# Two-block transformer kernel on one core: low query parts on 128 rows, pools at multiples of 128 bytes, one table load placed later

## The chip, the cores and the metric

The kernel runs on one core of a Trainium2 chip. A core has five engines that run beside each other, each with its own queue: TensorE (PE in the profile, with its weight loads shown apart as PEld), VectorE (DVE), ScalarE (ACT), GpSimd (POOL) and SyncE (SP, which issues most DMAs). Operands lie in SBUF, a memory of 128 partitions; matmul results lie in PSUM. The metric is the device time of one execution in microseconds, as the median of several runs.

## The reference

Two transformer blocks run one after the other on 512 tokens (and 256 context tokens in the first). Everything is float32. The first block has a gated delta network, a SwiGLU feed-forward, a differential attention and a second feed-forward. The second block has a layer with sliding-window and stick-breaking attention and a layer with a chunked recurrence (HGRN2), each followed by cross attention to 256 memory tokens and a feed-forward with a short convolution. The part that the change edits most is the differential attention:

```python
# q, k: two halves of 64 for each of 8 heads; keys of 512 tokens and 256 of the context
s = einsum('cbhqd,cbhkd->cbhqk', q, k)          # c = 0, 1: the two halves
p = softmax(s, axis=-1)
a = p[0] - lam_val * p[1]
o = einsum('bhqk,bhkv->bhqv', a, v)
out = rms_norm(o, subln_g) * (1 - lambda_init)  # then  w_out
# recurrence (HGRN2): log_f = log(lb + (1 - lb) * sigmoid(f_logit)); k = (1 - lb) * sigmoid(-f_logit)
```

## The kernel before

**Rounded pairs.** Nearly all products are made from operands that are split into a rounded high part and a low part (type F32R, fp32r in the profile): `h*h + h*l + l*h`, three matmuls instead of one float32 matmul. `weights` (L200 to L204) loads a raw weight unit `wr` of 128x1024 by DMA from SP, ScalarE casts it to `wh` (L203), VectorE subtracts to get `wl` (L204). Activations are split in the same way into tiles such as `h2h`/`h2l`, `h3h`/`h3l`, `fh`/`fl`, `f1h`/`f1l`, `b1h`/`b1l`. Every matmul goes through `mm` (L163), every transposition through `tr` (L167, with the identity `ident`), so the tile names tell them apart. One matmul streams 512, 384 or 256 columns of the moving operand past 128x128 stationary values. In the profile the first tile name of a matmul is the moving one, the second the stationary one: in `f1h,wh` an activation of 512 tokens moves past a 128x128 block of weights, in `wh,fh` 512 columns of weights move past a 128x128 block of the activation.

**Differential attention** (`diff_attention`, tiles of pool `da`). `project(pr)` makes keys, queries and values of a pair of heads. `ev_k` applies the rotation (`rope`, L1113 to L1116, which uses a tile `rot`) into the buffer `kraw` and splits it: for each half `cc` the tile `kx` holds the high part on the own 64 rows and the low part on the other 64. `ev_q` makes the rotated queries in a tile `qraw` and fills `q` of three planes: planes 0 and 1 hold, for each half, the high part on the own 64 rows and a second copy of it on the other 64 (L1130, L1131); plane 2 holds the low parts of both halves (L1132). So a score tile is made of two matmuls for each of four (half, key range) combinations: one over 128 rows, high times (high and low), and one over 64 rows, low times high:

```python
self.mm(s[cc][:, f, 0:384], q[:, cc, t * P:(t + 1) * P], kx[:, cc, fs], stop=False)
self.mm(s[cc][:, f, 0:384], q[cp, 2, t * P:(t + 1) * P], kx[cp, cc, fs], start=False)
```

There are 8 heads of 4 token tiles with 8 such matmuls, 256 in all, half of them over 64 rows. `attend` then takes maxima (L1182), exponentials (L1185), mixes the two halves (L1192), transposes the result (`a<-ident,p`) and multiplies with `v` (`o<-v,aT`). `head_norm_out` (L1228 to L1236) normalises a head in the tile `ho`. While one pair of heads is attended, `take` fills in matmuls of the next pair's projections, and in the last pair matmuls of the output projection. On each engine the instructions run in one order, which the build's planner fixes beforehand from the program's priorities.

**Pools.** SBUF tiles come from pools that are stacked from the left and from the right end of each partition. Tiles lie one behind the other in their pool at their own size. In the program as built, the left side begins at byte 16,512 of a partition (129 times 128) with the pool `const` of 5,728 bytes (44 times 128 and 96), so what lies behind it starts 96 bytes past a multiple of 128. The right side ends at byte 229,344 (96 past a multiple of 128), and the pool `ada` of 928 bytes below it leaves the next pools 64 past a multiple. Small tiles of one or a few numbers lie between large ones in several pools. Two of the operand pairs below: `wh` and `wl` lie at 64 past a multiple of 128 and `fh` of the last feed-forward too, `f1h` at 96 past; `h3h` lies at 64, and the normalised memory and queries of the cross attention (`mh`, `q0h`) lie at 0.

**Recurrence** (`hgrn_mixer`). L1873 takes an exponential of a 128x16 tile, `exp_ln_tables` (L160) loads ScalarE's table for exponential and logarithm, L1882 takes a logarithm `lno` of 128x8, and then for each 128 channels `ev_f` (L1928 to L1942) takes an absolute value, an exponential and a logarithm of 128x512.

Of the kernel before, what the change touches and what calls it, by code (L numbers as in the profile page):

```python
# [12 lines left out]
F32 = mybir.dt.float32  # L13
# [8 lines left out]
P = 128  # L22
D = 1024
NK = D // P
SEQ = 512
CTX = 256
TOK = SEQ + CTX
NT = SEQ // P
# [12 lines left out]
class Kernel:  # L41
# [19 lines left out]
    def __init__(self, ctx, tc, ins, out):  # L61
        self.ctx, self.tc, self.nc, self.i, self.out = ctx, tc, tc.nc, ins, out
        self.n = 0
        self.staged = []
        self.turns, self.rest = {}, None
        self.ada_own = 0


    def pool(self, name, bufs=1, space=None, side=None):
# [5 lines left out]
        return self.tc.alloc_tile_pool(name=name, bufs=bufs, reuse_waits="tile", **kw)  # L75
# [31 lines left out]
    def setup(self):  # L107
        nc = self.nc
        self.c = self.pool("const", side="left")
# [280 lines left out]
    def deltanet(self, xp, xT, scratch, zs, gts, later):  # L390
# [43 lines left out]
        hp = self.pool("dn_heads", side="right")  # L434
# [46 lines left out]
        pp = self.pool("dn_proj", side="left")  # L481
# [602 lines left out]
    def diff_attention(self, hh, hl, yh, yl, sb, spare, later, after):  # L1084
# [26 lines left out]
        def rope(dst, ps):  # L1111
            rot = one([P, SEQ], "rot", 1)
# [5 lines left out]
        def project(pr, out):  # L1118
# [4 lines left out]
            def ev_q(j, ps):  # L1123

                raw = one([P, SEQ], "qraw")
                rope(raw, ps[0])
                q[j] = one([P, 3, SEQ], "q", 2, F32R)
                for cc in range(2):
# [3 lines left out]
                    nc.vector.tensor_tensor(out=q[j][own, 2, :], in0=raw[own], in1=q[j][own, cc, :].bitcast(F32), op=SUB)  # L1132
# [34 lines left out]
        def attend(h, q, kx, v, work, steps):  # L1167
            po = self.bank("o")
            r0 = one([P, NT], "r0", 2)
            for t in range(NT):  # L1170
                s = [self.bank2() for _ in range(2)]
                for cc in range(2):
                    cp = slice(64 * cc, 64 * cc + 64)
# [122 lines left out]
    def first_block(self):  # L1296
        nc, i = self.nc, self.i
        self.ap = self.pool("ada", side="right")
        self.aw = self.pool("adaw", side="right")
        xp = self.pool("dn_x", side="right")  # L1300
        self.stage = self.pool("stage", 2, side="right")
# [111 lines left out]
        sb = self.pool("da", side="left")  # L1413
# [22 lines left out]
        sb.release()  # L1436
# [14 lines left out]
        self.stage = self.pool("stage", 2, side="right")  # L1451
# [83 lines left out]
    def ab_mixer(self, hh, hl, yh, yl, sb, done_h, fill):  # L1535
# [7 lines left out]
        at = self.pool("swa", side="right")  # L1543
# [8 lines left out]
        prep = self.pool("prep", side="right")  # L1552
# [53 lines left out]
        swp = self.pool("swt", side="right")  # L1606
# [80 lines left out]
        at = self.pool("stick", side="right")  # L1687
# [174 lines left out]
    def hgrn_mixer(self, hh, hl, yh, yl, sb, done_h, fill):  # L1862
# [18 lines left out]
        self.exp_ln_tables()  # L1881
        nc.scalar.activation(lno, olb, AF.Ln)  # L1882
# [34 lines left out]
        def project(pr):  # L1917
# [6 lines left out]
            def ev_f(j, ps):  # L1924
# [3 lines left out]
                nc.scalar.activation(a, ps[0], AF.Abs)  # L1928
# [331 lines left out]
```

## Time and profile before

| | us |
|---|---|
| median of 3 runs (3797.12 to 3800.86) | 3800.17 |
| the profiled execution's own time | 3806.98 |
| its span, first to last instruction | 3805.3 |
| PE busy in the span | 3681.0 (97%) |
| DVE, ACT, POOL busy | 2338.4, 1540.7, 436.5 |

The profile gives each engine's busy time, lines of instructions grouped by their place in the code, the chain of work that ended last, and a timeline in which a row is a start, a duration, the engine, the line and the tiles. A matmul's duration runs from its start to its modelled end in PSUM, and successive matmuls overlap; what one costs in a dense stretch is the distance from its start to the next one's start, called its step below. `PEclk` is the clock that TensorE was granted, 1.00 being 2.4 GHz.

### The profile page before, as it was taken

To read this page: it belongs to the slowest core of one execution; us is meant where nothing else is said; L and a number is where in the kernel's file an instruction comes from. 1 tells how busy PE (TensorE), PEld (TensorE's weight loads), DVE (VectorE), ACT (ScalarE), POOL (GpSimd) and SP (SyncE) were. 2 spreads that over 40 slices of the span, in tenths; PEclk is the share of its full clock that TensorE was granted. 3 is DMA by queue.
4 is the path that set the end of the run, shared out by engine and by line. 5 is a ranking of instruction groups with operands and counts; after the bars stand their busy time and mean duration, and the time that the engine had idled before them with its cause. 6 is when DMAs were issued, how large, how long until landed. Compare 5 with 4: busy or idle time off the path is not lost.

```text
span 3805.3 us, 57443 instructions
## 1 busy us (share of the span) xinstructions
PE 3681.0 (97%) x23195; PEld 3032.8 (80%) x23195; DVE 2338.4 (61%) x3919; ACT 1540.7 (40%) x2834; POOL 436.5 (11%) x642
## 2 busy tenths in 40 slices
PE   8999998999999999999999999999999999999999
PEld 5776777888888787777888877888887878888887
DVE  4757765633444766677555656556666776556665
ACT  4445444321111344443222456543334555444332
POOL 3112220130000110003000202100001122100000
PEclk8999999999999999999999999999999999999999
DMA  4234334422222211113333213223232223212322
GB/s 168 89 98 143 116 120 145 136 67 61 67 62 61 74 45 40 45 40 108 95 94 100 78 53 98 63 66 100 89 100 78 78 68 102 93 61 89 95 94 83
DMA packets 246667, 329.44 MB, mean 87 GB/s; under 512 B 12103, under 2 KB 192683, under 8 KB 246400
## 3 DMA queue, kind: packets, MB, share of 16 engines
q1 hardware_dynamic: 245696, 325.39, 27.2%
q8 instruction: 182, 2.98, 0.3%
q14 instruction: 85, 0.70, 0.1%
q0 software_dynamic: 704, 0.37, 0.0%
HBM read 318.09 MB, written 7.63 MB: 86 GB/s over the span
## 4 chain that ended last, share of the span: by engine, by line
PE 82%; DVE 7%; ACT 4%; POOL 3%; DMA 2%; issue 2%; SPq 0%; ACTq 0%; POOLq 0%; DVEq 0%
PE g L163 41%; PE a L163 14%; PE o L163 13%; PE s L163 7%; PE i L163 2%; DMA araw<-in_ada_w_dram 1%; PE s L167 1%; PE a L167 1%; PE p L163 1%; DVE wl L204 1%; ACT wh L203 1%; ACT xr L1476 1%; ACT Wt L721 0%; DVE bst L964 0%; ACT xr L1473 0%
## 5 line engine op out<-in xcount | busy, mean ns | idle before, releaser
L204 DVE TENSOR_TENSOR wl<-wr,wh 128x1024 fp32r<-128x1024 f32 (+1 forms) x508 | 585.4, 1160 | 441.7 <-ACT wh L203 428.0
L203 ACT CAST wh<-wr 128x1024 fp32r<-128x1024 f32 (+1 forms) x508 | 493.4, 980 | 768.7 <-PE o L163 386.7
L163 PE MATMUL g<-wh,fh 128*128 128x512 f32 x396 | 156.4, 396 | 0.0
L163 PE MATMUL g<-wh,fl 128*128 128x512 f32 x396 | 156.0, 395 | 0.0
L163 PE MATMUL g<-wl,fh 128*128 128x512 f32 x396 | 155.1, 392 | 0.0
L163 PE MATMUL g<-h2l,wh 128*128 128x512 f32 x352 | 138.0, 392 | 2.5 <-DVE h2l L1010 2.5
L163 PE MATMUL g<-h2h,wh 128*128 128x512 f32 x352 | 137.5, 392 | 0.0
L163 PE MATMUL g<-h2h,wl 128*128 128x512 f32 x352 | 137.2, 390 | 0.0
L152 POOL TENSOR_SCALAR brs<-bmv 128x1 f32<-128x1 f32 x20 | 9.7, 484 | 937.1 <-DVE bmv L966 928.0
L163 PE MATMUL g<-hh,wh 128*128 128x512 f32 (+1 forms) x376 | 112.4, 358 | 3.4 <-ACT hh L417 1.6
L163 PE MATMUL g<-hl,wh 128*128 128x512 f32 (+1 forms) x376 | 111.0, 354 | 1.8 <-POOL hl L418 1.7
L163 PE MATMUL g<-hh,wl 128*128 128x512 f32 (+1 forms) x376 | 110.2, 354 | 1.7 <-DVE wl L204 1.7
L1045 DVE TENSOR_TENSOR x<-g,x 128x512 f32<-128x512 f32 x120 | 82.5, 688 | 31.0 <-PE g L163 30.8
L163 PE MATMUL s<-k,q 128*128 128x384 f32 (+1 forms) x256 | 98.7, 440 | 0.0
L1182 DVE TENSOR_REDUCE nm<-s 128x1 f32<-128x768 f32 x64 | 61.1, 955 | 52.4 <-PE s L163 52.3
L163 PEld LDWEIGHTS g<-wh,fh 128*128 128x128 f32 x396 | 74.4, 188 | 17.4 <-ACT fh L2092 0.6
L1287 ACT CAST fh<-sg 128x768 fp32r<-128x768 f32 (+1 forms) x44 | 32.0, 727 | 139.0 <-DVE sg L1286 139.0
L163 PEld LDWEIGHTS g<-wl,fh 128*128 128x128 f32 x396 | 74.4, 188 | 16.6
L163 PEld LDWEIGHTS g<-wh,fl 128*128 128x128 f32 x396 | 74.4, 188 | 16.4 <-DVE fl L2093 0.4
L1286 DVE TENSOR_TENSOR sg<-g,sg 128x512 f32<-128x512 f32 x33 | 22.8, 691 | 98.0 <-PE g L163 98.0
L163 PEld LDWEIGHTS g<-hh,wh 128*128 128x128 f32 x376 | 62.7, 193 | 24.7 <-issue 9.3
L163 PEld LDWEIGHTS g<-hh,wl 128*128 128x128 f32 x376 | 62.5, 192 | 23.7 <-issue 13.2
(992 smaller groups left out, 11541.2 us busy)
## 6 DMA issues: line engine op xcount, KB each, us to landing
wr<-in_ffn_w_up_dram SPq DMA_DIRECT2D x132, 512.0 KB, 3.6
araw<-in_ada_w_dram SPq DMA_DIRECT2D x48, 1024.0 KB, 5.2
wr<-in_ffn_w_down_dram SPq DMA_DIRECT2D x88, 512.0 KB, 3.7
wr<-in_ffn_w_gate_dram SPq DMA_DIRECT2D x44, 512.0 KB, 3.8
wr<-in_dn_w_in_dram SPq DMA_DIRECT2D x66, 256.0 KB, 4.4
wr<-in_xa_w_kv_dram SPq DMA_DIRECT2D x32, 512.0 KB, 3.5
wr<-in_hgrn_w_in_dram SPq DMA_DIRECT2D x32, 512.0 KB, 3.8
wr<-in_da_w_in_dram SPq DMA_DIRECT2D x24, 512.0 KB, 3.5
```

The costliest lines, as they stand in the source:

```text
L152: nc.gpsimd.tensor_scalar(out=out, in0=in_, scalar1=mul, scalar2=add, op0=MUL, op1=ADD)
L163: self.nc.tensor.matmul(out, lhsT=lhsT, rhs=rhs, start=start, stop=stop)
L167: self.nc.tensor.transpose(out, in_, self.ident[0:k, 0:k])
L203: nc.scalar.copy(hi, raw)
L204: nc.vector.tensor_tensor(out=lo, in0=raw, in1=hi.bitcast(F32), op=SUB)
L1045: nc.vector.tensor_tensor(out=a, in0=ps, in1=a, op=ADD)
L1182: nc.vector.tensor_reduce(out=nm, in_=s[cc][:, :, 0:384], axis=AX.XY, op=MAX, negate=True)
L1286: nc.vector.tensor_tensor(out=s, in0=p[:, 0:n], in1=s, op=MUL)
L1287: nc.scalar.copy(hi[j], sg[j])
L1476: nc.scalar.activation(y, x, AF.Copy, scale=rs)
```

## The change

It does three things, and some that these need.

1. In the differential attention, `q` gets four planes: the low part of each half has a plane of its own, with zeros (set by GpSimd) on the other 64 rows, and the low matmul runs over 128 rows. The tile `qraw` is gone, its work is done in `kraw`; the tile `rot` is gone, its work is done in a buffer of the tag `ho`.
2. Pools are brought to multiples of 128 bytes (32 numbers). `const` and `ada` get 32 and 64 bytes of padding. In pools that are not marked `packed`, each tile's size is rounded up to 128 bytes; in the pools `da`, `mix` and `xa`, tiles under 32 numbers go to a small pool beside.
3. In the recurrence, the table load and the logarithm `lno` come behind the first absolute value in `ev_f`.

```diff
+LINE = 32
     def t(self, pool, shape, tag, dt=F32, bufs=None):
+
         self.n += 1
-        return pool.tile(shape, dt, tag=tag, name=f"{tag}_{self.n}", bufs=bufs)
+        name = f"{tag}_{self.n}"
+        n = math.prod(shape[1:])
+        if n < LINE:
+            pool = self.small.get(id(pool), pool)
+        if id(pool) in self.packed or n % LINE == 0:
+            return pool.tile(shape, dt, tag=tag, name=name, bufs=bufs)
+        x = pool.tile([shape[0], -(-n // LINE) * LINE], dt, tag=tag, name=name, bufs=bufs)[:, 0:n]
...
+    def pool_pair(self, name, side):
+
+        pool = self.pool(name, side=side)
+        self.small[id(pool)] = self.pool(name + "s", side=side, packed=True)
+        return pool
...
+    def fill_lines(self, pool, n):
+
+        pad = self.t(pool, [P, n], "pad")
+        self.nc.gpsimd.memset(pad, 0.0)
...
-        self.c = self.pool("const", side="left")
+        self.c = self.pool("const", side="left", packed=True)
+        self.fill_lines(self.c, 8)
...
         def rope(dst, ps):
-            rot = one([P, SEQ], "rot", 1)
+            rot = one([P, NT, P], "ho", 1).rearrange("p t d -> p (t d)")
...
-                raw = one([P, SEQ], "qraw")
+
+                raw = kraw[:, 0:SEQ]
                 rope(raw, ps[0])
-                q[j] = one([P, 3, SEQ], "q", 2, F32R)
+                q[j] = one([P, 4, SEQ], "q", 2, F32R)
...
-                    nc.vector.tensor_tensor(out=q[j][own, 2, :], in0=raw[own], in1=q[j][own, cc, :].bitcast(F32), op=SUB)
+                    nc.gpsimd.memset(q[j][other, 2 + cc, :].bitcast(F32), 0.0)
+                    nc.vector.tensor_tensor(out=q[j][own, 2 + cc, :], in0=raw[own], in1=q[j][own, cc, :].bitcast(F32), op=SUB)
...
-                        self.mm(s[cc][:, f, 0:384], q[cp, 2, t * P:(t + 1) * P], kx[cp, cc, fs], start=False)
+                        self.mm(s[cc][:, f, 0:384], q[:, 2 + cc, t * P:(t + 1) * P], kx[:, cc, fs], start=False)
...
-        self.ap = self.pool("ada", side="right")
+        self.ap = self.pool("ada", side="right", packed=True)
+        self.fill_lines(self.ap, 16)
...
-        sb = self.pool("da", side="left")
+        sb = self.pool_pair("da", "left")
...
-        self.exp_ln_tables()
-        nc.scalar.activation(lno, olb, AF.Ln)
...
                 nc.scalar.activation(a, ps[0], AF.Abs)
+                if k == 0:
+                    self.exp_ln_tables()
+                    nc.scalar.activation(lno, olb, AF.Ln)
                 nc.scalar.activation(a, a, AF.Exp, scale=-1.0)
```

## Rows read from the trace of the kernel before

**Rows 1.** The page: span, busy time of each engine, chain that ended last.
```profile
span 3805.3 us, 57443 instructions
PE 3681.0 (97%) x23195; PEld 3032.8 (80%) x23195; DVE 2338.4 (61%) x3919; ACT 1540.7 (40%) x2834; POOL 436.5 (11%) x642
...
PE 82%; DVE 7%; ACT 4%; POOL 3%; DMA 2%; issue 2%; SPq 0%; ACTq 0%; POOLq 0%; DVEq 0%
```

**Rows 2.** Busy time by stretches: us, then each engine's busy, clock, DMA share, GB/s.
```profile
1357.00:1700.00 343.00, 336.20 (x1916) 267.39 (x1915) 224.85 (x419) 161.47 (x333) 17.61 (x24) 0.99 0.13 41
1640.00:1700.00 60.00, 56.76 (x276) 41.84 (x277) 39.47 (x79) 30.50 (x72) 3.96 (x6) 0.91 0.06 18
1760.00:2000.00 240.00, 240.00 (x1071) 197.46 (x1071) 133.03 (x153) 63.08 (x76) 6.40 (x7) 1.00 0.33 98
2700.00:2900.00 200.00, 200.00 (x865) 162.31 (x864) 135.57 (x180) 63.83 (x85) 0.00 (x0) 1.00 0.30 95
```

**Rows 3.** Score matmuls by form, 1357 to 1700: count, busy us, mean ns.
```profile
L163 PE MATMUL s<-k,q 64*128 64x384 f32 x128 | 57.3, 447 | 0.0
L163 PE MATMUL s<-k,q 128*128 128x384 f32 x128 | 55.4, 433 | 0.0
```

**Rows 4.** Weight loads in time, one half's scores: start, duration, idle before.
```profile
1401.22 0.19 PEld L163 LDWEIGHTS g<-wl,h3h 128*128 128x128 f32 x1
1401.35 0.46 PEld L167 LDWEIGHTS a<-ident,p 128*128 128x128 f32 x4
1401.78 0.19 PEld L163 LDWEIGHTS s<-k,q 128*128 128x128 f32 x1
1402.16 0.18 PEld L163 LDWEIGHTS s<-k,q 64*128 64x128 f32 x1 [0.18 <-issue]
1402.53 0.19 PEld L163 LDWEIGHTS s<-k,q 128*128 128x128 f32 x1 [0.19 <-issue]
1402.90 0.18 PEld L163 LDWEIGHTS s<-k,q 64*128 64x128 f32 x1 [0.19 <-issue]
1403.27 0.20 PEld L167 LDWEIGHTS a<-ident,p 128*128 128x128 f32 x2 [0.19 <-issue]
```

**Rows 5.** Timeline of PE in the last feed-forward, 512 columns.
```profile
3720.23 0.39 PE L163 MATMUL g<-wl,fh 128*128 128x512 f32 x1
...
3722.27 0.39 PE L163 MATMUL o<-wl,fh 128*128 128x512 f32 x1
3722.49 0.40 PE L163 MATMUL g<-f1h,wh 128*128 128x512 f32 x1
...
3726.00 0.40 PE L163 MATMUL g<-f1h,wh 128*128 128x512 f32 x1
```

**Rows 6.** Timeline of PE, 256 columns: values projection, then cross attention's queries.
```profile
1400.02 0.28 PE L163 MATMUL g<-wh,h3h 128*128 128x256 f32 x1
...
1401.34 0.28 PE L163 MATMUL g<-wl,h3h 128*128 128x256 f32 x1
...
2435.27 0.28 PE L163 MATMUL g<-wl,q0h 128*128 128x256 f32 x1
...
2449.40 0.28 PE L163 MATMUL o<-wl,q0h 128*128 128x256 f32 x1
```

**Rows 7.** Timeline of PE: the first and the last of the dense rounded matmuls.
```profile
37.99 0.51 PE L163 MATMUL g<-hh,wl 128*128 128x512 f32 x2
...
3799.93 0.39 PE L163 MATMUL o<-wh,fl 128*128 128x512 f32 x1
```

**Rows 8.** Timeline of PE: two plain float32 matmuls of 512 columns, operands at 0.
```profile
118.72 1.02 PE L163 MATMUL i<-gi,gt 128*128 128x512 f32 x2
```

**Rows 9.** The same form's durations, min/median/max in ns.
```profile
L163 PE MATMUL i<-gi,gt x32: 377/537/595, 118.7 to 513.0; 128*128 128x512 f32 x16, 128*128 128x256 f32 x16
```

**Rows 10.** Timeline of POOL and ACT in the recurrence: a 128x512 fill, the table loads.
```profile
2931.82 0.53 POOL L1885 MEMSET keep<- 128x512 f32 x1
...
2941.81 1.28 ACT L1873 ACT_TABLE_LOAD   x1
2943.11 0.21 ACT L1873 ACTIVATE lexp<-lexp 128x16 f32<-128x16 f32 x1
2943.34 1.28 ACT L160 ACT_TABLE_LOAD   x1
2944.63 0.21 ACT L1882 ACTIVATE lno<-olb 128x8 f32<-128x8 f32 x1
2944.83 0.60 ACT L1928 ACTIVATE fa<-g 128x512 f32<-128x512 f32 x1
```

**Rows 11.** The chain that ended last, around one head's normalisation.
```profile
1417.52 0.70 DVE ho L1228
...
1424.35 0.63 PE a L167 x4
```

More of the change, by code (lines that the diff above doesn't have):

```diff
@@ L64, in __init__, with pool @@
         self.staged = []
+        self.packed, self.small = {}, {}
         self.turns, self.rest = {}, None
         self.ada_own = 0
-    def pool(self, name, bufs=1, space=None, side=None):
+    def pool(self, name, bufs=1, space=None, side=None, packed=False):
         kw = {}
@@ L433, in deltanet @@
         self.ada_own = self.ada_bufs
-        hp = self.pool("dn_heads", side="right")
+        hp = self.pool("dn_heads", side="right", packed=True)
         one = lambda shape, tag, bufs=1, dt=F32: self.t(hp, shape, tag, dt, bufs)
@@ L480, in deltanet @@
         W2 = SEQ + 4 + CTX
-        pp = self.pool("dn_proj", side="left")
+        pp = self.pool("dn_proj", side="left", packed=True)
         onep = lambda shape, tag, bufs=1: self.t(pp, shape, tag, F32, bufs)
@@ L1297, in first_block @@
         nc, i = self.nc, self.i
-        self.ap = self.pool("ada", side="right")
-        self.aw = self.pool("adaw", side="right")
-        xp = self.pool("dn_x", side="right")
-        self.stage = self.pool("stage", 2, side="right")
+        self.ap = self.pool("ada", side="right", packed=True)
+        self.fill_lines(self.ap, 16)
+        self.aw = self.pool("adaw", side="right", packed=True)
+        xp = self.pool("dn_x", side="right", packed=True)
+        self.stage = self.pool("stage", 2, side="right", packed=True)
         self.ada_setup()
@@ L1435, in first_block @@
         ln.release()
-        sb.release()
+        self.release_pair(sb)
         yTp.release()
@@ L1450, in first_block @@
         g, b = self.load_bc(ln, i["ln2_g"][1], "g"), self.load_bc(ln, i["ln2_b"][1], "b")
-        self.stage = self.pool("stage", 2, side="right")
+        self.stage = self.pool("stage", 2, side="right", packed=True)
         self.load_ffn_cols()
@@ L1542, in ab_mixer @@
         vb = one([P, NT, 512], "vb")
-        at = self.pool("swa", side="right")
+        at = self.pool("swa", side="right", packed=True)
         on = lambda shape, tag, bufs=1, dt=F32: self.t(at, shape, tag, dt, bufs)
@@ L1551, in ab_mixer @@
         va = on([P, NT, P], "va")
-        prep = self.pool("prep", side="right")
+        prep = self.pool("prep", side="right", packed=True)
         pr = lambda shape, tag, bufs=1, dt=F32: self.t(prep, shape, tag, dt, bufs)
@@ L1605, in ab_mixer @@
         self.exp_ln_tables()
-        swp = self.pool("swt", side="right")
+        swp = self.pool("swt", side="right", packed=True)
         on = lambda shape, tag, bufs=1, dt=F32: self.t(swp, shape, tag, dt, bufs)
@@ L1686, in ab_mixer @@
         at.release()
-        at = self.pool("stick", side="right")
+        at = self.pool("stick", side="right", packed=True)
         on = lambda shape, tag, bufs=1, dt=F32: self.t(at, shape, tag, dt, bufs)
@@ L2110, in second_block @@
             yTp, yh, yl = self.new_h(f"my{l}", SEQ, "right")
-            sb = self.pool("mix", side="right")
+            sb = self.pool_pair("mix", "right")
             kv = []
@@ L2122, in done_h @@
                 kvp = self.pool("kv", side="left")
-                mp = self.pool("memh", side="left")
+                mp = self.pool("memh", side="left", packed=True)
                 kT = self.t(kvp, [P, NK, 256], "mkT")
@@ L2152, in second_block @@
             yTp, yh, yl = self.new_h(f"cy{l}", SEQ, "right")
-            sb = self.pool("xa", side="right")
+            sb = self.pool_pair("xa", "right")
             w_o, part = i["xa_w_o_2"][l], self.xa_part
```

18 lines of the change are left out of this document (14 added, 4 removed).

## Prediction

> **What bounds the kernel now.** I read the page first. TensorE is busy for 3681.0 of 3805.3 us, no other engine for more than 61%, and the chain that ended last lies on PE for 82% [rows 1]. A busy PE need not be an efficient one, because matmuls overlap, so I then read stretches: in two feed-forwards PE has no idle time at all while DVE is busy for 133.03 of 240 us and 135.57 of 200 us, and in the differential attention PE is busy for 336.20 of 343 us with DVE at 224.85 [rows 2]. So what shortens the distance between matmul starts shortens the kernel, up to the point where VectorE or a chain through it comes last. The timeline of PE gives that distance, in two places where the change works.
>
> First, the scores. The table by form shows 128 matmuls over 64 rows and 128 over 128 rows, with 447 and 433 ns from start to modelled end [rows 3]. The weight loads show their steps: 1401.78, 1402.16, 1402.53, 1402.90, 1403.27, that is 372 ns from one to the next, and before each the weight loader is idle for 0.18 to 0.19 us with nothing that the profile can name [rows 4]. The loads before them, all over 128 rows, have no such gap. Here the forms alternate 128, 64, 128, 64. A change of rows thus seems to make the load wait for the matmul before it: 0.19 idle and 0.18 load is the whole step.
>
> Second, the dense rounded matmuls. With 512 columns, the nine steps from 3720.23 to 3722.27 take 226.7 ns each, and the 15 from 3722.49 to 3726.00 take 234.0 ns, on the same engine at the full clock, one after the other, with nothing waited for [rows 5]. In the first stretch both operands lie 64 bytes past a multiple of 128; in the second, the moving one lies 96 past. With 256 columns, 11 steps from 1400.02 to 1401.34 take 120.0 ns (both at 64), and 120 steps from 2435.27 to 2449.40 take 117.8 ns (moving at 64, stationary at 0) [rows 6]. One column per cycle at 2.4 GHz would be 213.3 and 106.7 ns. So 226.7 is 213.3 and 13.4, 120.0 is 106.7 and 13.3: the excess does not grow with the columns, and it is just 32 columns, or 128 bytes, of the moving operand. That is what reading one more piece of 128 bytes (17 for 16, 9 for 8) would cost. No rounded operand moves from a multiple of 128 anywhere in this kernel, so the trace has no row of the state after.
>
> **The sum, part by part.** All against the profiled execution (3806.98 us, span 3805.3 us).
>
> *Alignment.* I counted the steps between successive rounded matmuls over the whole timeline, from 37.99 to 3799.93 us [rows 7], leaving out those over 40 ns above one column per cycle: 8,498 with 512 columns (mean 230.8 ns) and 6,428 with 256 (mean 119.0); 1,129 more are longer, ended by waits, and are left as they are. What is the step when both operands start at a multiple of 128? The upper bound is no gain. The lower is one column per cycle. The nearest row is a plain float32 matmul with operands at 0: two of 512 columns take 1.02 us [rows 8], one alone 0.595 at most [rows 9], so the step is 0.425 or a little over, against 426.7 for two cycles per column: next to nothing besides its columns, with a weight load of its own each time. I take 2.5 ns over the columns: 215.8 and 109.2. That is 8,498 x 15.0 = 127 us and 6,428 x 9.8 = 63 us, together 190 us. Not all of it arrives: the feed-forwards should give it in full, while in mixers and normalisations a step that is saved partly turns into a longer wait. I take 85%, 162 us, with 70% (133) and 100% (190) as bounds.
>
> *Low parts on 128 rows.* The 256 score matmuls take 97.0 us from start to start (379 ns on average, the 372 of [rows 4] and some longer ends). If none changes rows any more they should step like the others: 384 columns are 160 ns, with 2.5 that is 162.5, so 256 x 0.1625 = 41.6 us and 55 us less. With 13.3 over the columns it would be 44.4 and 53 us less. The stage has cover: PE falls from 336 to about 270 us (some 11 us of alignment included) with DVE's 225 below it, but DVE is then at 83%, and in the last pair (1640 to 1700) PE already has 3.2 us idle and a clock of 0.91 [rows 2], so there the maxima and exponentials come next. I take 80%, 44 us, bounds 25 and 55.
>
> *What that adds.* 16 fills of 64x512 on POOL; the nearest row is a fill of 128x512 with 0.53 us [rows 10], so 8.5 us at most over a stage in which POOL is busy for 17.61 of 343 us. A head's `hms` steps queue behind them; 0.53 us twice for each of 8 heads would be 8 us if PE had nothing else, but it has projections to fill in: 0. The fills at the start are smaller still: 0.
>
> *Shared buffers.* With `rot` in `ho`, a rotation can't start while a head's normalisation holds the buffer, from 1417.52 to 1424.98, 7.5 us [rows 11]; before, a rotation could start inside that time. The shuffle would wait on DVE with maxima and weight splits behind it. Six heads have rotations beside them. With `kraw` also used for queries, a query's rotation waits for the last key's split, at most some 2 us, 4 times a pair. Bounds 0 and 6 x 7.5 + 16 x 2 = 77 us; the planner places a rotation when it is ready and other projections lie between, so I take the low end, inside the 20% above.
>
> *Table load.* The two loads of 1.28 us, the 0.21 us logarithm and the first absolute value of 0.60 us run back to back on ACT [rows 10]; the absolute value moves ahead of the second load and the exponential behind it still waits for the load. 0, bounds 1.5 us either way.
>
> Sum: 162 + 44 = 206 us. 3806.98 - 206 = 3601; the median of the runs shown lies 6.8 us under the profiled execution, so 3594, rounded to 3595. With the bounds, 190 + 55 = 245 gives 3555 and 133 + 35 = 168 gives 3632.
>
> **A rule against it.** The two stretches of [rows 5] differ only in which bytes the operands start at, 64 or 96 past a multiple of 128, and differ by 7.3 ns a step. The Trainium skill, page "SBUF — State Buffer", section "Specifications (TRN2)", gives lines of 16 bytes; by that alone 64 and 96 are as good as 0 and alignment would bring nothing. By that rule, the trace disagrees already, in those rows.
>
> The weight loads over 128 rows start while the matmul before them runs, all through [rows 4] outside the scores. The page "TensorE: Matmul & The Clock Gate" of the Trainium skill, section "Part 3: Packing small matmuls", says that a load overlaps running matmuls only if its row groups differ. By that rule, scores on equal rows would not get faster; the rows of equal form, at 120 ns a step with loads of 0.19 us, speak against it.
>
> **The rivals.**
>
> *Only the stationary side or the mismatch matters.* The one comparison with an operand at 0 is the stationary one in [rows 6]: 2.2 ns, not 10. If that is all, steps settle at 10.8 ns over the columns: 224.1 and 117.5. That saves 69 us over the same steps, and with 44 for the scores the time is 3687, to 3720 if only the 96s come down to the 64s. For it: it is all that the trace shows. Against: the excess of exactly 128 bytes at both widths.
>
> *Alignment does nothing.* Then 44 us remain: 3756. Against it stand the two stretches of [rows 5].
>
> *The scores don't speed up,* because the load waits for something other than the change of rows: 3638.
>
> *The padding misses.* If a pool's size is still off, what lies behind it keeps its steps; with about half the steps aligned, 81 + 44 gives 3675. The sums speak against it: 96 + 32 and, from the top, 96 - 928 - 64 are multiples of 128, and rounded tiles keep it so.
>
> *Slower.* The shared `ho` buffer puts DVE behind the head's chain through POOL: up to 77 us as above. It decides only where alignment brings nothing and the waits exceed the 44 us of the scores, some 4 us for each of 12 rotations. At its worst: 3800 - 44 + 77 = 3833. Rotations today start without such waits, and the chance that all of this meets is small.
>
> **How the numbers follow.** Forecast 0.60 (3555 to 3632); stationary side or mismatch 0.22 (3687 to 3720); alignment nothing 0.06; scores unchanged 0.05; padding misses 0.05; slower 0.02. The range of 3560 to 3715 holds nearly all of the forecast and of the stationary case, and the scores and padding cases, above 0.8. A change of 0.2%, 7.6 us, is about what a measurement of this kernel can tell from none. Faster has all but the last case and a margin: 0.97; same 0.01; slower 0.02.
>
> **What would show it.** In the trace after, steps of 512 and 256 columns near 216 and 109 in the feed-forwards; if they read 224 and 118 it was the stationary side. Score weight loads without the 0.19 idle and about 165 ns apart. DVE's rotation shuffle in the attention with or without waits for PE's `ho` transposition. PE's idle time and granted clock in the last pair's stretch. The forecast is wrong if the excess of 13 ns is a fixed cost of changing weights at full rate, or if idle time on PE grows by more than some 60 us.

## The result, and the profile after

The changed kernel takes 3743.91 us (median of 4, 3742.61 to 3745.88) where the kernel before took 3800.52 on the same chip: a ratio of 0.9848 [0.9836, 0.986], 57 us less. The forecast was 3595 with a range of 3560 to 3715, so the time lies 29 us above the range. The direction was right; the gain was little more than a quarter of the one foretold.

The page of the changed kernel: span, busy time of each engine, chain that ended last.

```profile
span 3740.9 us, 57477 instructions
PE 3614.9 (97%) x23195; PEld 3032.0 (81%) x23195; DVE 2331.9 (62%) x3919; ACT 1539.5 (41%) x2833; POOL 444.3 (12%) x660
...
PE 81%; DVE 7%; ACT 5%; POOL 3%; issue 2%; DMA 2%; SPq 0%; ACTq 0%; POOLq 0%; DVEq 0%
```

Against [rows 1], PE is busy for 66.1 us less in a span that is 64.4 us shorter, with as many matmuls; the other engines changed by 8 us at most. PE's idle time stayed (124 and 126 us). So the gain is PE's, and it is in the steps, not in the waits.

**Scores.** Busy time by stretches of the changed kernel (us; busy time and count of PE, PEld, DVE, ACT, POOL; granted clock, DMA share, GB/s): the differential attention and its last pair, as in the first two lines of [rows 2]; the score matmuls by form; and PE's weight loads in one half's scores (start, duration).

```profile
1359.00:1647.30 288.30, 277.34 (x1806) 247.40 (x1805) 210.57 (x401) 151.92 (x317) 20.23 (x32) 0.99 0.14 45
1590.00:1650.00 60.00, 55.22 (x332) 47.29 (x331) 47.58 (x99) 35.66 (x87) 4.13 (x7) 0.94 0.11 36
```

```profile
L196 PE MATMUL s<-k,q 128*128 128x384 f32 x256 | 59.7, 360 | 0.2
```

```profile
1389.89 1.42 PEld L196 LDWEIGHTS o<-v,aT 128*128 128x128 f32 x12
1391.22 0.65 PEld L196 LDWEIGHTS s<-k,q 128*128 128x128 f32 x4
1391.86 0.19 PEld L196 LDWEIGHTS g<-wh,h3h 128*128 128x128 f32 x1
```

Four score loads now stand in 0.65 us, with no idle time between, where [rows 4] show one in 0.37 us with 0.19 idle ahead of each. From start to start the 256 score matmuls take 57.2 us, not 96.9: 185 of them step in 174.9 ns, the other 71, most at the end of a group, in 350 on average. In the last pair PE is busy for 55.22 of 60 us and DVE for 47.58, and the clock is 0.94 where it was 0.91.

**Dense steps.** PE's timeline in the last feed-forward, as [rows 5]: first `fh`, then `f1h`; and one with 256 columns, as the second pair of [rows 6].

```profile
3654.66 0.39 PE L196 MATMUL g<-wl,fh 128*128 128x512 f32 x1
...
3659.42 0.39 PE L196 MATMUL o<-wl,fh 128*128 128x512 f32 x1
3659.65 0.39 PE L196 MATMUL g<-f1h,wh 128*128 128x512 f32 x1
...
3666.90 0.39 PE L196 MATMUL a<-f1h,wl 128*128 128x512 f32 x1
```

```profile
2385.01 0.28 PE L196 MATMUL o<-wh,q0h 128*128 128x256 f32 x1
...
2387.86 0.28 PE L196 MATMUL g<-wh,q0h 128*128 128x256 f32 x1
```

The 21 steps on `fh` take 226.7 ns each, as before, though both operands now lie at a multiple of 128 and not 64 past it. The 32 on `f1h` take 226.6, down from 234.0. The 24 with `q0h` take 118.8, up from 117.8. So the dear steps came down to the cheap ones, and the cheap ones stayed where they were within 1 ns. Over the whole timeline, counted as in the prediction, the steps of 512 columns went from 1961.5 to 1935.7 us, those of 256 from 764.9 to 766.5, the scores from 96.9 to 57.2: together 63.9 us, beside 64.4 us of the span. The medians give 57 us: the profiled execution of the kernel before lies 6.5 us above its median, that of the changed kernel 1.3 us under, so the match with the span holds for these two executions.

### The profile page after: what moved, and what is told of

Same layout as the page of the kernel before. It is cut to its first block, busy times and chain, and to the rows that moved or that the text cites. A ratio compares the mean times of both kernels' runs of the same rounds, so it can differ in the third digit from the quotient of the medians.

```text
span 3740.9 us, 57477 instructions
## 1 busy us (share of the span) xinstructions
PE 3614.9 (97%) x23195; PEld 3032.0 (81%) x23195; DVE 2331.9 (62%) x3919; ACT 1539.5 (41%) x2833; POOL 444.3 (12%) x660
## 4 chain that ended last, share of the span: by engine, by line
PE 81%; DVE 7%; ACT 5%; POOL 3%; issue 2%; DMA 2%; SPq 0%; ACTq 0%; POOLq 0%; DVEq 0%
PE g L196 41%; PE a L196 15%; PE o L196 13%; PE s L196 6%; PE i L196 2%; PE s L200 1%; PE a L200 1%; PE p L196 1%; DMA araw<-in_ada_w_dram 1%; DVE wl L237 1%; ACT wh L236 1%; ACT xr L1511 1%; ACT hsq L1267 1%; POOL hms L189 0%; ACT Wt L754 0%
## 5 line engine op out<-in xcount | busy, mean ns | idle before, releaser
L196 PEld LDWEIGHTS g<-hh,wl 128*128 128x128 f32 x376 | 63.0, 193 | 24.0 <-issue 13.3
L196 PEld LDWEIGHTS g<-h2h,wl 128*128 128x128 f32 x352 | 66.2, 188 | 13.5
L196 PEld LDWEIGHTS g<-h2l,wh 128*128 128x128 f32 x352 | 66.4, 189 | 13.2 <-DVE h2l L1043 1.0
```

What stands on the lines that cost most here:

```text
L196: self.nc.tensor.matmul(out, lhsT=lhsT, rhs=rhs, start=start, stop=stop)
```

## The experiments

**The parts one by one.** What each part brings was tried first, by undoing one part of the change or doing one part alone.

Low parts on 128 rows, in the kernel before, with the shared buffers that they need:

```diff
-                        self.mm(s[cc][:, f, 0:384], q[cp, 2, t * P:(t + 1) * P], kx[cp, cc, fs], start=False)
+                        self.mm(s[cc][:, f, 0:384], q[:, 2 + cc, t * P:(t + 1) * P], kx[:, cc, fs], start=False)
```

> The kernel before with the score part alone: four planes of q, low parts on 128 rows with zeros, and the shared buffers; no padding, table load where it was. If the score part is worth what the changed kernel's score steps say (97.0 to 57.2 us), the time is 40 us under the kernel before, 3760. If the padding also helped the scores, or the shared buffers cost something that the padding hid, it is less: 3775 or more. The prediction's own figure for this part is 44 us, 3756.

3768.97 us, 0.9907 [0.9893, 0.9922]: 35 us, with the scores at 57.1 us. The rest of the steps kept their size.

The changed kernel with that line undone:

```diff
-                        self.mm(s[cc][:, f, 0:384], q[:, 2 + cc, t * P:(t + 1) * P], kx[:, cc, fs], start=False)
+                        self.mm(s[cc][:, f, 0:384], q[cp, 2 + cc, t * P:(t + 1) * P], kx[cp, cc, fs], start=False)
```

> The changed kernel with the low score matmuls over 64 rows again (from their own planes); padding, zeros, shared buffers and table load as in the changed kernel. If the parts add up, the time is about 24 us under the kernel before, 3776: the rounded matmuls of 512 columns take 25.8 us less from start to start, those of 256 columns 1.6 us more. If the zeros and shared buffers cost something, the time lies higher, up to 3790. By the prediction's theory alignment alone would have been 3638.

3783.38 us, 0.9945 [0.9931, 0.996]: 21 us remain for the padding with the moved table load. 35 and 21 are 56 of the 57 us, so these two parts add up. (The table load is taken apart further down.)

The shared buffers alone, in the kernel before (`rot` in `ho`, `qraw` in `kraw`):

> The kernel before with the shared buffers alone: rotation in a buffer of the tag ho, query rotation in kraw; scores over 64 rows, no padding. If the planner places rotations between the heads' normalisations, the time is that of the kernel before within 2 us. If a rotation waits behind a head's chain, up to 7.5 us for each of six heads and 2 us for each of 16 rotations, it is slower; the scores-only kernel lay some 4 us above what its score steps give, so 4 us slower would settle where that went.

3802.69 us, 1.0001 [0.9992, 1.001]. They cost nothing, and the forecast's bound of 77 us for them falls.

**Which offsets matter.** A kernel of its own, run once, with 24 matmuls of each kind, back to back, their operands shifted in their tiles (the cut shows the shift and the matmul):

```diff
+        v = x[:, OFFS[o]:OFFS[o] + n]          # 0, 16, 32, 64, 96 bytes
+        nc.tensor.matmul(acc[:, b, 0:n], lhsT=s[rows, (j % 2) * 128:(j % 2) * 128 + 128], rhs=m[rows, 0:n],
```

> A small kernel that does none of the reference's work: 24 rounded matmuls in a row for each pair of byte offsets (moving, stationary) past a multiple of 128, at 512 and at 256 columns, then 384 columns with operands on all 128 rows, on rows 0 to 63, on rows 64 to 127, and alternating. Theory P (the prediction's): at (0,0) a step is 215.8 and 109.2 ns, any other moving offset adds one piece of 128 bytes, 13 ns. Theory F (formed on the changed kernel's trace, where 512 columns at (0,0) still step by 227): the 13 ns are paid by every rounded matmul wherever it lies, (0,0) equals (64,64) with 226.7 and 120.0. Within F, theory M: what adds to 226.7 is a difference of 32 between the two offsets (231 to 238), and (32,32) and (96,96) step like (0,0). Theory O: an offset that isn't a multiple of 64 costs by itself, so that (32,32) steps like (32,0). Both leave 64 against 0 at 224 and 117.5. Rows: if a change of rows is what costs, 128 rows in a row and 64 rows in a row both step by 173 at 384 columns, and the alternations of 128 with 64 rows by about 370; if 64 rows cost by themselves, 64 rows in a row step by 370 too.

With 512 columns, operands both at a multiple of 128 stepped in 232.3 ns, both at 64 in 231.9, both at 32 in 232.4; the moving one at 64 and the stationary at 0 in 229.2; all others between 231.7 and 234.1. So a multiple of 128 is nothing special, but neither did equal offsets give the 227 ns that the kernels show for them.

Next, the changed kernel with the right side's pools moved to 64 past a multiple of 128, the left side's left at 0 (its edit is the cut), and then the changed kernel with all pools at 32 past one (other sizes of the same padding):

```diff
-        self.fill_lines(self.ap, 16)
+        self.fill_lines(self.ap, 32)
```

> The changed kernel with 64 bytes more padding in the pool ada, so that all that is stacked from the right lies at 64 past a multiple of 128 and all that is stacked from the left at 0. 4,008 matmuls of 512 columns and 3,168 of 256 then have operands 64 apart. If a difference of 64 bytes saves 2.3 ns a step at 256 columns (as cross attention's queries had it before) and the same at 512, the time is 14 to 17 us under the changed kernel, 3728. If only a stationary operand at 0 with a moving one at 64 gains, it is some 8 us. If the offset of 64 has no bearing at 512, 3740. By the theory that only multiples of 128 are good it would be slower than the changed kernel by up to 25 us.

3753.59 us, 0.9859 [0.9843, 0.9876]: nothing gained on the changed kernel, and by the dense steps of the two profiled executions 11.5 us lost (17.3 more with 512 columns, 5.8 less with 256). Operands 64 apart, in either direction, cost up to 6 ns a step with 512 columns and give back 2 to 5 with 256.

> The changed kernel with every pool 32 bytes past a multiple of 128 instead of 0, all operands alike (32, 32). Theory M (only a difference between the two offsets costs): 512 columns at 227.8, the time of the changed kernel, 3744. Theory O (an offset that is no multiple of 64 costs by itself): 8,500 steps 3 to 6 ns longer, 3770 to 3795. Before, the operands at (96, 96) stepped by 232.7 on average, but only in the first stage, where 512 and 256 columns alternate.

3742.14 us, 0.984 [0.9826, 0.9853], as the changed kernel: the lines of 128 bytes, on which the forecast stood, have no part in it. What is left to look at is the distance of the two operands.

Then a kernel that was to use it, with matching offsets (64 and 64) for most steps of 512 columns, and 64 apart for many of 256:

```diff
+        if name in ("f0", "f1"):
+            self.nc.gpsimd.memset(p.tile([P, 16], F32, tag="pad", name=f"pad_{name}"), 0.0)
...
-        self.fill_lines(self.ap, 16)
+        self.fill_lines(self.ap, 32)
...
+        nc.gpsimd.memset(sb.tile([P, 16], F32, tag="pad", name=f"pad_{self.n}"), 0.0)
```

> The changed kernel with the pools on the right at 64 past a multiple of 128 bytes, and on the left the FFN's pools (hidden parts and normed input) at 64 as well, the other pools on the left at 0. So the two operands agree for most steps of 512 columns, and 2,784 steps of 256 columns have them 64 apart, for which the run with the right side at 64 showed 116.1 ns where the changed kernel has 119.4. Sum: 256 columns -6 us, 512 columns +1 to +3 us for the 768 that still differ: 3 to 5 us under the changed kernel, 3737 to 3742. If the gain at 256 columns is not the offset's, the time is that of the changed kernel.

3757.67 us, 0.9876 [0.9863, 0.9889], by the ratios 11 us above the changed kernel. It missed, and its rows say why: `f0h,wh`, both 64 past a multiple of 128, stepped in 233.3 ns, `h4h,wh`, both 64 past one too, in 226.9. In bytes of the partition, modulo 256, the first pair lies at 64 and 192, the second at 192 and 192. So take as distance the address of the moving operand less that of the stationary one, in bytes and modulo 256: 128 for the first pair, 0 for the second. Sorted by it, the dense steps between two rounded matmuls of one width fall into place in these four kernels (ns, with the count):

| distance | 0 | 64 | 96 | 128 | 160 | 192 |
|---|---|---|---|---|---|---|
| 512 columns: before | 227.9 (4149) | | 233.3 (1370) | | 234.2 (2340) | |
| changed | 227.4 (7873) | | | | | |
| right side at 64 | 227.9 (4093) | 229.1 (2341) | | | | 233.4 (1447) |
| the kernel above | 227.7 (4087) | 229.7 (421) | | 232.9 (3202) | | 233.0 (163) |
| 256 columns: before | 119.6 (2959) | 117.4 (1351) | 119.9 (1151) | | 118.8 (332) | |
| changed | 119.7 (4444) | | | 119.0 (1346) | | |
| right side at 64 | 119.6 (2985) | 117.1 (1680) | | | | 114.9 (1157) |
| the kernel above | 119.6 (2959) | 117.4 (1343) | | 118.9 (332) | | 114.1 (1147) |

That is a reading after the fact. Three runs tested it. First a map, a kernel of its own that was run once, one distance after the other (the cut is its loop):

```diff
+            c = o + 128 * ((j // 3) % 4)
+            nc.tensor.matmul(bank[j % 2][:, 0:n], lhsT=w[:, c:c + 128], rhs=x[:, 0:n], start=True, stop=True)
```

> Does none of the reference's work. 24 matmuls each of 512 and of 256 columns, rounded float32, every one with its own weight load, the stationary operand moved in steps of 16 bytes against the moving one: all 16 distances modulo 256, and 256 and 384 bytes further. Theory D (only the distance of the two operands in a partition, modulo 256 bytes, sets the step): at 512 columns 227 ns at 0 and again 256 bytes further, 229 to 230 at 64, 232 to 234 at all others, 128 among them; at 256 columns 120 at 0, 117 at 64, 114 at 192, 119 at 128. Rival M (modulo 128): the step at 128 is that at 0, and that at 192 is that at 64.

Busy time by stretches of 24 matmuls: 512 columns at distances 0, 192, 128, 64, 0 and 128 (the last two 256 bytes further), then 256 columns at 0 and 192.

```profile
19.52:24.96 5.44, 5.44 (x26) 4.50 (x24) 0.00 (x0) 0.00 (x0) 0.00 (x0) 1.00 0.00 0
41.59:47.19 5.60, 5.60 (x26) 4.51 (x24) 0.00 (x0) 0.00 (x0) 0.00 (x0) 1.00 0.00 0
63.96:69.56 5.60, 5.60 (x25) 4.50 (x24) 0.00 (x0) 0.00 (x0) 0.00 (x0) 1.00 0.00 0
86.27:91.77 5.50, 5.50 (x26) 4.51 (x24) 0.00 (x0) 0.00 (x0) 0.00 (x0) 1.00 0.00 0
108.42:113.87 5.45, 5.45 (x26) 4.50 (x24) 0.00 (x0) 0.00 (x0) 0.00 (x0) 1.00 0.00 0
113.87:119.46 5.59, 5.59 (x26) 4.52 (x24) 0.00 (x0) 0.00 (x0) 0.00 (x0) 1.00 0.01 3
119.46:122.31 2.85, 2.85 (x25) 2.85 (x24) 0.00 (x0) 0.00 (x0) 0.00 (x0) 1.00 0.00 0
130.82:133.55 2.73, 2.73 (x27) 2.73 (x26) 0.00 (x0) 0.00 (x0) 0.00 (x0) 1.00 0.02 6
```

The first number after the stretch, divided by 24, is the step: 226.7 at 0 (5.44), 233.3 at 128 and 192 (5.60), 229.2 at 64 (5.50), and again 227 and 233 when 256 bytes further on. With 512 columns distances 0, 16 and 240 step in 226.7 to 227.0, 64 and 80 in 228.7 and 229.8, the other eleven in 232.0 to 234.1. With 256 columns 192 stands out (2.73, and 113.3 inside the stretch); the rest lies between 116.7 and 120.1. The two operands of the first micro kernel turn out to have been 128 apart wherever their offsets were equal, so its 232 ns at equal offsets agree with the map. (The Trainium skill, page "SBUF — State Buffer", section "Specifications (TRN2)", gives lines of 16 bytes; by that alone distances of 0 and 128 would cost the same, and the map has 226.7 and 233.3: a line of 16 bytes does not explain these steps.)

At two distances the two micro kernels disagree. The first one also had 24 matmuls of 512 columns at 16, then 24 at 240:

```profile
91.30:96.86 5.56, 5.56 (x25) 4.51 (x24) 0.00 (x0) 0.00 (x0) 0.00 (x0) 1.00 0.00 0
96.87:102.46 5.59, 5.59 (x26) 4.53 (x25) 0.00 (x0) 0.00 (x0) 0.00 (x0) 1.00 0.00 0
```

That is 231.7 and 233.0 ns, where the map has 227.0 and 226.7. So the distance does not set the step alone. The kernels differ in the order of their operands too. And in the first stage of the changed kernel, where matmuls of 512 and of 256 columns take turns and the table does not count them, the 491 of 512 columns at distance 0 step in 232.6 ns (232.2 in the kernel before): what comes next counts as well. What sets these steps stays open. No rounded matmul of 512 or 256 columns of the real kernels lies at 16 or 240; at 64, 96, 128, 160 and 192 the two micro kernels agree within 1.5 ns.

Then the changed kernel with every operand still at a multiple of 128, but 3,240 of its matmuls of 512 columns 128 apart (`shift` puts so many unused numbers ahead of a pool's tiles):

```diff
+        self.shift(p, {"f0": 32, "f1": 32}.get(name))
...
+        self.shift(sb, 32)
```

> The changed kernel with the normed input of the last two FFNs and the hidden parts of the first two 128 bytes further on: every operand still lies at a multiple of 128 bytes, but 3,240 of the 8,928 matmuls of 512 columns and 384 more of 256 now have their two operands 128 apart modulo 256. Theory D: some 3,200 dense steps at 232.9 for 227.4 ns, +17.6 us, so 3759 to 3763 us by the changed kernel's 3744. Rival M (multiples of 128 bytes are enough, as the change has it): as the changed kernel, 3742 to 3746.

3761.76 us, 0.9884 [0.9868, 0.9901], as the distance modulo 256 had it and outside the interval of the changed kernel; the span is 19.2 us longer. PE's timeline in its last feed-forward, first `fh`, then `f1h`:

```profile
3675.76 0.39 PE L201 MATMUL g<-wh,fl 128*128 128x512 f32 x1
...
3677.34 0.39 PE L201 MATMUL o<-wl,fh 128*128 128x512 f32 x1
3677.57 0.40 PE L201 MATMUL g<-f1h,wh 128*128 128x512 f32 x1
...
3687.83 0.40 PE L201 MATMUL a<-f1h,wl 128*128 128x512 f32 x1
```

The 7 steps on `fh` take 226 ns, the 44 on `f1h` 233.2: nearly the 234.0 of [rows 5] again, with both operands at multiples of 128. So what helped in the padding is not that operands lie at multiples of 128, but that its tiles' sizes happened to bring all 8,928 pairs of 512 columns to a distance of 0 modulo 256.

Last, the distances chosen by the map:

```diff
+        self.shift(p, {"f0": 48, "f1": 48, "q0": 32, "q1": 32, "dy": 16}.get(name))
...
-        self.fill_lines(self.ap, 16)
+        self.fill_lines(self.ap, 32)
...
+        self.shift(sb, 48)
```

> The changed kernel with its pools set by the distance of the operands modulo 256 bytes: 8,160 of 8,928 matmuls of 512 columns stay at 0, 2,592 of 7,128 matmuls of 256 columns go to 192 and 768 to 64. Theory D: some 2,350 dense steps of 256 columns at 114.4 for 119.4 ns, -11.7 us, 690 at 117.2 for 119, -1.3 us, some 420 of 512 columns at 229.7 and 163 at 233.2 for 228.5, +1.3 us: 11 to 12 us under the changed kernel, 3730 to 3735 us, a ratio of 0.9818. Rival M: as the changed kernel or, with the offsets no longer equal, above it, 3744 to 3756.

3735.36 us (3732.43 to 3742.33), 0.9822 [0.9807, 0.9836]. The steps did nearly what was foretold: 2,310 of 256 columns at distance 192 took 115.2 ns, and all steps of 256 columns 756.9 us, 9.6 less than in the changed kernel. That it beats the changed kernel is likely but not settled: the intervals touch (0.9836), and its profiled execution, the longest of its four, has the changed kernel's span (3740.6). In that one the first 457 us took 4.7 us longer, and the rest 5.0 less.

**What the 13 ns are.** A kernel of its own, run once, with all operands at distance 0, 48 matmuls of each kind (the cut is its loop):

```diff
+            s, m = ((h, 0), (h, 1), (l, 0))[0 if same else j % 3]
+            nc.tensor.matmul(bank[j % banks][0:cols, 0:n], lhsT=s[r, 128 * w:128 * w + cols], rhs=x[m][r, 0:n],
```

> A small kernel that does none of the reference's work: stretches of 48 matmuls at offset 0 for moving and stationary operands, in the order high-high, high-low, low-high of the real kernel, to see on what the 13 ns over the columns depend. ka, kb: rounded, 512 and 256 columns, one PSUM bank. kc: two banks in turn, each matmul a sum of its own. kd: the same stationary operand every time. ke, kf: the same order with 2-byte operands (bfloat16). kg, kk: 64 and 32 stationary columns. km, ko: eight matmuls of 384 columns alternating between 128 rows and rows 0 to 63, rounded and in 2 bytes, each amid dense ones. Theory W (the excess is the exchange of the stationary operand): ka 226.7, kb 120.0, ke and kf the same excess or one that shrinks with the bytes, kg and kk a smaller excess. Theory R (the excess belongs to reading 4-byte moving operands at full rate): ka 226.7, ke and kf near 216 and 109, kg and kk as ka. If the banks matter, kc is slower than ka. Rows: km near 370 a step as in the kernel before; ko the same if the change of rows costs whatever the type.

Stretches of 48 matmuls (columns as above): rounded float32 of 512 columns, of 256, of 512 with the same stationary block each time, then bfloat16 of 512 and of 256, then rounded with 64 stationary columns; and two of 8 matmuls of 384 columns in turn on 128 and 64 rows, rounded and bfloat16.

```profile
19.59:30.47 10.88, 10.88 (x49) 9.02 (x48) 0.00 (x0) 2.49 (x5) 0.00 (x0) 1.00 0.01 2
30.47:36.22 5.75, 5.75 (x49) 5.75 (x48) 0.00 (x0) 0.00 (x0) 0.00 (x0) 1.00 0.00 0
47.13:58.02 10.89, 10.89 (x50) 8.84 (x48) 0.00 (x0) 0.00 (x0) 0.00 (x0) 1.00 0.01 2
58.02:68.39 10.37, 10.37 (x50) 4.71 (x50) 0.00 (x0) 0.00 (x0) 0.00 (x0) 1.00 0.00 0
68.39:73.55 5.16, 5.16 (x50) 4.63 (x48) 0.00 (x0) 0.00 (x0) 0.00 (x0) 1.00 0.01 3
73.55:84.66 11.11, 11.11 (x51) 6.51 (x49) 0.00 (x0) 0.00 (x0) 0.00 (x0) 1.00 0.00 0
115.03:117.89 2.86, 2.86 (x10) 1.31 (x9) 0.00 (x0) 0.00 (x0) 0.00 (x0) 1.00 0.00 0
126.32:128.46 2.14, 2.14 (x10) 0.76 (x9) 0.00 (x0) 0.00 (x0) 0.00 (x0) 1.00 0.03 8
```

The steps inside are 226.7, 120.0, 226.7, 215.8, 109.2 and 230.0 ns. At this distance bfloat16 steps 2.5 ns above one column per cycle, rounded float32 13.3 at both widths, whether or not the stationary values change, and not less with fewer of them. So at distance 0 the excess belongs to the operands' type and not to the exchange of the stationary values. It is no fixed sum: with 256 columns at distance 192 the map has 113.3 ns, only 6.6 over the columns. Bfloat16 was run at distance 0 alone, so whether placement counts for it is not shown, and what in rounded float32 costs 13.3 ns stays open.

In the last two stretches the change of rows costs a step of 369 ns in rounded float32 and 267 in bfloat16, against 160 for the columns. In the first micro kernel 48 matmuls of 384 columns over 64 rows each, 24 on rows 0 to 63 and then 24 on rows 64 to 127, took 8.10 us, 169 ns each: it is the turn that costs, not the 64 rows. It also had the turns at length (24 matmuls on 128 rows and rows 0 to 63, then 24 on 128 rows and rows 64 to 127), and there the granted clock of the stretch fell to 0.74, then 0.50:

```profile
151.80:159.90 8.10, 8.10 (x50) 7.81 (x49) 0.00 (x0) 0.00 (x0) 0.00 (x0) 1.00 0.01 2
159.90:171.10 11.20, 11.20 (x25) 5.38 (x24) 0.00 (x0) 0.00 (x0) 0.00 (x0) 0.74 0.00 0
171.10:185.30 14.20, 14.20 (x24) 6.58 (x23) 0.00 (x0) 0.00 (x0) 0.00 (x0) 0.50 0.00 0
```

**The table load.** The changed kernel with the load and `lno` back at their old place:

```diff
+        self.exp_ln_tables()
+        nc.scalar.activation(lno, olb, AF.Ln)
...
-                if k == 0:
-                    self.exp_ln_tables()
-                    nc.scalar.activation(lno, olb, AF.Ln)
```

> The changed kernel with the table load and the logarithm lno back where they were, ahead of the recurrence's loops. The prediction says the move is worth 0, at most 1.5 us either way: the same time as the changed kernel within its interval, a ratio of 0.984 to 0.986 to the kernel before. If the load's place moves the planner's order around it, a few us off.

3771.09 us, 0.9913 [0.99, 0.9927]: 29 us above the kernel with all pools at 32 (3742.14 us) and by the ratios 25 above the changed kernel, where the forecast had 0. ScalarE's timeline of this kernel, in three places:

```profile
2447.05 0.22 ACT L1908 ACTIVATE lexp<-lexp 128x16 f32<-128x16 f32 x1 [2.38 <-DVE lexp L1907]
2447.29 1.28 ACT L193 ACT_TABLE_LOAD   x1
...
2525.89 1.28 ACT L2122 ACT_TABLE_LOAD   x1
2527.18 0.63 ACT L2122 ACTIVATE cg<-cg 128x512 f32<-128x512 f32 x1
...
2890.00 1.28 ACT L1964 ACT_TABLE_LOAD   x1
2891.29 0.63 ACT L1964 ACTIVATE fa<-fa 128x512 f32<-128x512 f32 x1
2891.83 1.03 ACT L236 CAST wh<-wr 128x1024 fp32r<-128x1024 f32 x1
2892.88 1.28 ACT L1965 ACT_TABLE_LOAD   x1
2894.18 0.63 ACT L1965 ACTIVATE fa<-fa 128x512 f32<-128x512 f32 x1
```

In [rows 10] the exponential of `lexp` and the load stand right ahead of the recurrence. With the padding they run some 440 us ahead of it; the feed-forward's activation (L2122) then loads another table, and from 2890.00 on exponentials and logarithms each load one of their own, 31 times by 3120, 1.28 us each, many of them in the chain that ended last: ScalarE is busy for 149.45 of the 220 us from 2890 to 3110 where the changed kernel has 125.00.

```profile
2890.00:3110.00 220.00, 194.10 (x2266) 167.67 (x2264) 150.52 (x249) 149.45 (x237) 40.25 (x65) 0.96 0.21 63
```

```profile
2890.00:3110.00 220.00, 207.74 (x2478) 180.46 (x2477) 172.75 (x288) 125.00 (x236) 44.59 (x70) 1.00 0.22 69
```

The first line is of this kernel, the second of the changed one. Three runs tested the reading. First, a second load behind the first activation, all else as in this kernel:

```diff
                 nc.scalar.activation(a, ps[0], AF.Abs)
+                if k == 0:
+                    self.exp_ln_tables()
```

> The changed kernel with the table load and lno back at the old place, and a second load of the same table behind the recurrence's first activation. Theory G: the second load alone gives back the 29 us, so the time is that of the changed kernel within 4 us (3741 to 3748) with 28 or 29 table loads. Rival N (the place of lno, or the order of the work, costs the 29 us): about 3771 us.

3747.15 us, 0.9847 [0.9832, 0.9862], with 28 loads: the second load gives all of it back. Second, the padding with neither the rows nor the moved load:

> The changed kernel with the low score matmuls on 64 rows and the table load with lno at its old place: padding and shared buffers alone. In the run with only the table load put back ScalarE loaded tables 58 times and not 27, and the span was 29 us longer. Theory G (the padding gives the small tiles a pool of their own, the prologue with the table load then runs some 490 us ahead of the recurrence, and another function's table replaces it): 58 loads here too, of them 28 in the recurrence, and a span of 3782 + 29 = 3811 us, 3 to 10 us above the kernel before. Rival N (the 29 us belong to the whole change's order of work): about 28 loads and 3783 us, as with the load moved.

3808.93 us, 1.001 [1.0001, 1.002], with 58 loads: on its own the padding is worth nothing, its 21 us and a little more go to the table loads. Third, the moved load in the kernel before:

> The kernel before with only the table load and lno moved behind the first activation of the recurrence. Theory G: without the pool of small tiles the prologue stays where it was, right ahead of the recurrence, 28 loads as before, and the time is that of the kernel before within 3 us. Rival: the load of 1.28 us leaves the path or joins it at each of its places, and the time still changes by less than 0.1%; if it moves by 5 us or more, the move does something that neither theory has.

3806.07 us, 1.0 [0.9992, 1.0008], with 28 loads: without the padding it is worth nothing. That the earlier start comes from the small pool beside `mix`, which leaves these tiles nothing to wait for, is the likeliest reason; it was not tried apart from the rest of the padding.

## Why the prediction was wrong, step by step

*Alignment, 162 us: wrong, the step that failed.* It read the excess of 13.3 ns as one more piece of 128 bytes, because 13.3 ns is just 32 columns, and took the plain float32 matmuls of [rows 8] for the state after. The excess is there at a multiple of 128 too (226.7 ns), with all operands 32 past one as well, and in a kernel with nothing else to do. What moved was the distance of the operands: 25.8 us less with 512 columns, 1.6 more with 256, and 21 us of it in the time.

The trace of the kernel before had a row against this step. [rows 8] showed plain float32, which takes two cycles a column, and there the excess is small wherever the operands lie. The 96 plain float32 matmuls `i<-qk` have both operands at 0, 16, 32 and so on up to 112 past a multiple of 128, and the same typical duration at each of the eight:

```profile
L163 PE MATMUL i<-qk x96: 377/379/483, 124.6 to 546.4; 128*128 128x256 f32 x96
```

In the changed kernel the matmuls of [rows 8] have their operands at 64 and 32 past a multiple of 128, and still step in 428 to 432 ns. So [rows 8] said something about the type, not about the offset 0.

The text named the failing case itself ("a fixed cost ... at full rate"), and gave it no time or chance of its own; that the cost is one of changing weights did not hold either (226.7 ns with the same stationary block). The rival of the mismatch came nearest to the mechanism, though equal offsets modulo 128 were not enough. Its end of 3720 missed by 24 us: it took 36 us for the 96s, where the padding brought 21, and 44 for the scores, which brought 35. The range ended at 3715, short even of that end. That rival's other end has a slip: 117.8 ns in [rows 6] is 11.1 over the columns and not 10.8, so its steps would save some 62 us, not 69, and give 3694. The nearest number, 3756 of "alignment does nothing", was near by luck: placement did bring 21 us, and the scores fell short by 9.

*Low parts on 128 rows: right in kind, mis-sized.* The wait at a change of rows was real and is gone. The term counted every score at 162.5 ns, or 173 with the excess; 185 of 256 took 174.9, and the 71 others 350. So 40 us left the steps, not 55, and 35 arrived, within the bounds of 25 and 55. (The rule of the Trainium skill weighed there, page "TensorE: Matmul & The Clock Gate", section "Part 3: Packing small matmuls", asks for other row groups if a load is to overlap, and beside that names only a background weight buffer; the rows show the reverse of the rule, four loads on equal rows in 0.65 us and a turn of rows at 369 ns.)

*Cover in the attention: right.* DVE is busy for 210.57 of 288.3 us, in the last pair for 47.58 of 60, where PE has 55.22: DVE did not become the limit.

*Fills, shared buffers:* the buffers alone cost nothing (1.0001), so 0 was right and the 77 us of the bound were not there. The fills were never run alone; with them the score part brought 35 of the 40 us that left its steps, so if they cost anything it is hardly more than those 5.

*Table load: 0 held in the kernel before (1.0), and in the changed kernel its bounds of 1.5 us were wrong.* The step looked at the load where [rows 10] had it. The padding moves what stands ahead of it, and not moving the load would have cost 25 to 29 us. The step asked what the moved load passes, not what the other parts make of its old place.

*Slower, 3833:* the shared buffer did not hold anything up. What did cost time, the padding with the load at its old place (1.001 without the score part), no rival had.

## What to carry to other kernels

Before an excess per instruction is put down to where operands lie, compare types and the distance between the two operands: here rounded float32 at distance 0 costs 13.3 ns a matmul whether its operands lie at a multiple of 128 bytes or 32 or 64 past one, where bfloat16 costs 2.5, and placement moves a step by up to 7 ns with the distance modulo 256 bytes. A rule that fits two numbers and needs a state that no row shows deserves a chance well under a half, and a micro kernel of some twenty matmuls can test it. A preloaded table holds only until a function runs that loads another one (L2122 here), so count the table loads in the trace whenever tiles get pools of their own or become ready earlier.

## What the runs showed of the hardware that was not expected

The step of a rounded matmul of 512 columns depends on the distance of its operands in the partition. In the map it repeats 256 bytes further on: 226.7 ns at 0, about 229 at 64 and 80, and 232 to 234 nearly everywhere else; at 16 and 240 the map has 227 and another kernel 232 to 233, and at 0 a matmul that is followed by one of 256 columns took 232 to 233, so the distance is not all. With 256 columns the best distance is another one: 113.3 ns at 192, against 119 to 120 at 0. Why is open. Matmuls in turn on 128 and 64 rows take 369 ns for 384 columns, and in the longest such stretch the granted clock was 0.50, the 1.2 GHz of its two levels, after it had been 1.00 on equal rows.
